# Two output tiles of a weight half, matmul by matmul in turn instead of one after the other

## The chip, the core and the metric

One core of a Trainium2 chip runs the whole kernel. The time is device microseconds of one execution. All times below come from the timed runs or from one profiled execution of the kernel before. The engines are named as in the profile: PE is TensorE's matmul, PEld its weight load, DVE is VectorE, ACT is ScalarE, POOL is GpSimd, SP is SyncE.

## The reference

One layer of a hybrid decoder on 336 tokens (16 meta tokens, 256 of a prompt, 8 sequences of 8 new ones), width 2048. Cut to what matters:

```python
def swiglu(x, wg, wu, wd):
    return (jax.nn.silu(x @ wg) * (x @ wu)) @ wd

def layer(h, st, p, lead):
    h = h + 0.5 * swiglu(rmsnorm(h, ...), w_gate, w_up, w_down)     # 2048 -> 5632 -> 2048
    z = rmsnorm(h, ...) @ w_in                                       # 2048 -> 8200
    y_s5, ... = s5_mixer(z[..., :o0], ...)                           # complex diagonal state space
    y_ml, ... = mlstm_mixer(...)                                     # matrix memory, 4 heads
    gates = sigmoid(z[..., o5:])
    merged = gates[..., :D] * (y_s5 @ w_branch_s5) + gates[..., D:] * (y_ml @ w_branch_mlstm)
    h = h + merged @ w_out
    h = h + 0.5 * swiglu(rmsnorm(h, ...), w_gate, w_up, w_down)
```

Everything is float32, and the outputs are the normed rows and the new states.

## The kernel before, in words

Activations lie by feature: a tile holds 128 features on the partitions and the tokens (336 in FFN 1 and the first part of the mixer, 320 after) along the free dimension. A float32 product is made of three matmuls of type float32r: high part of the weights times high part of x, high times low, low times high.

`Weights` (L47) brings the weights in the order of their use, in loads of 1 MB on SP's queue. Each load gives two halves of four k tiles by 256 columns. `_split` (L86) makes the two parts of a half: ACT copies `whi` (L95), DVE subtracts to get `wlo` (L96). `take` (L115) is called before a half's matmuls and splits two halves ahead (AHEAD = 2); four buffers each hold `whi` and `wlo`.

`product` (L380) adds one half to two PSUM tiles `ps[0]` and `ps[1]`, one for each 128 of its 256 columns. These are called column tile 0 and column tile 1 here. The matmuls are those of L388, L389 and L390, 24 to a half. After each column tile it calls `tick` (L407), which takes a step of the generators that run beside the products: `tick(0)` of those in `self.fast` alone, `tick(1)` of all in `self.bg`. The generator `s5_parameters` (in FFN 1, with `s5_weights`, L677, whose matmuls L751, L764 and L765 use small PSUM tiles) and `mlstm` (L1123) are in `fast`; `s5` (L1308), `v_turn` and others are not.

`pair` (L426) takes two PSUM tiles from the pool `psm` (four buffers, tag mm, in rotation; `mm_psum`, L142) and runs one to four halves into them. Small work uses another pool of four (`sm_psum`).

`ffn` (L432) goes over 11 blocks of 512 hidden features, each with two rounds `pr`. A round is a pair pg (gate, four halves) and a pair pu (up, four halves), and then `gated` (L438) for column tile 0 and for column tile 1:

```python
            nc.vector.tensor_tensor(gs, pg, self.rstd, op=ALU.mult)      # L443
            nc.scalar.activation(gs, gs, AF.Silu)                        # L444
            nc.vector.tensor_tensor(us, pu, self.rstd, op=ALU.mult)      # L445
            nc.vector.tensor_tensor(us, us, gs, op=ALU.mult)             # L446
            nc.scalar.copy(ah, us)                                       # L447
            nc.vector.tensor_tensor(al, us, ah.bitcast(F32), op=ALU.subtract)  # L448
```

The first round of each FFN uses the small pool for pg and pu; the other 21 use the mm pool. After the first round of a block comes `down` (L450) of the block before: eight pairs of one half each, after each of which `add` (L454) has DVE add both tiles to h (L457). At the end of FFN 1 the parts of the next norm are made as well (`ffn_done`, L330, L338). The mixer (L777) uses `pair` with two or four halves, and what reads its tiles is posted one to three halves later (`post`, L404).

The order of each engine's instructions is written out by the program (`manual_schedule`): an engine takes them as the Python code issues them.

Of the kernel before, what the change touches and what calls it, by code (L numbers as in the profile page):

```python
# [13 lines left out]
P = 128  # L14
# [32 lines left out]
class Weights:  # L47
    """The weights in the order in which TensorE takes them: loads of 1 MB, each cut into two halves
    of four k tiles by 256 columns, and each half split exactly into two float32r parts."""

# [51 lines left out]
    def first(self, part):  # L102
        """The first half, two k tiles at a time."""
        if part == 0:
            self.half[0] = tuple(self.k.wsp.tile([P, 4, 256], F32R, tag=t, name=t) for t in ("whi", "wlo"))
        s = slice(2 * part, 2 * part + 2)
        hi, lo = (t[:, s] for t in self.half[0])
        src = self.raw[0][:, s]
        self.k.nc.scalar.copy(hi, src)
        self.k.nc.vector.tensor_tensor(lo, src, hi.bitcast(F32), op=ALU.subtract)  # L110
        if part == 1:
            self.done[0] += 1
            self.split += 1
# [9 lines left out]
class Kernel:  # L123
# [43 lines left out]

# [1 line left out]
    def plan(self):  # L169
# [56 lines left out]

# [1 line left out]
    def constants(self):  # L228
# [89 lines left out]

# [1 line left out]
    def norm_begin(self, hi_slot, lo_slot, n, gain):  # L320
# [33 lines left out]

# [1 line left out]
    def load_x(self):  # L356
# [3 lines left out]
    def x_features(self, j):  # L360
        """Four tiles of x, turned and split; to be called again for what h takes from PSUM."""
        nc, xs = self.nc, self.xs
        tiles = []
        for m in range(4 * j, 4 * j + 4):
            ps = self.mm_psum()
            s = slice(P * m, P * m + P)
            nc.tensor.transpose(ps[:, 16:144], xs[0][:, s], self.ident)
            nc.tensor.transpose(ps[:, 144:272], xs[1][:, s], self.ident)
            nc.tensor.transpose(ps[:, 272:336], xs[2][0:64, s], self.ident[0:64, 0:64])
            nc.tensor.transpose(ps[:, 0:16], xs[2][64:80, s], self.ident[64:80, 64:80])  # L370
            self.norm_split(m, ps[:, 0:NT])
            tiles.append((m, ps))
            if m == 1:
                yield
        yield
        for m, ps in tiles:
            nc.vector.tensor_copy(self.h[:, m], ps[:, 0:NT])

# [1 line left out]
    def product(self, ps, half, xh, xl, k0, first, last, ks=range(4)):  # L380
        """Adds to the two PSUM tiles a half's four k tiles by its 256 columns."""
        nc = self.nc
        hi, lo = half
        for m in range(2):
            c = slice(P * m, P * m + P)
            for k in ks:
                a, b = xh(k0 + k), xl(k0 + k)
                nc.tensor.matmul(ps[m], hi[:, k, c], a, start=first and k == 0, stop=False)  # L388
                nc.tensor.matmul(ps[m], hi[:, k, c], b, start=False, stop=False)  # L389
                nc.tensor.matmul(ps[m], lo[:, k, c], a, start=False, stop=last and k == 3)  # L390
            if ks[-1] == 3:
                self.tick(m)

    def take(self):
        """The next half, and what was put off until now."""
        half = self.w.take()
        self.now += 1
        due = [x for x in self.posted if x[0] <= self.now]
        self.posted = [x for x in self.posted if x[0] > self.now]
        for _, fn in due:  # L400
            fn()
        return half
# [4 lines left out]
    def tick(self, m=1):  # L407
        """Takes what runs beside the large products a step further: at every half, and what is in
        fast at each of its two columns of tiles."""
        for g in list(self.bg):  # L410
            if m == 0 and g not in self.fast:
                continue
            try:
                next(g)
            except StopIteration:
                self.bg.remove(g)
# [122 lines left out]

# [1 line left out]
    def s5_parameters(self):  # L541
        nc, i = self.nc, self.ins
        v, s = nc.vector, nc.scalar
# [9 lines left out]
        at = [0]  # L553
# [21 lines left out]
        ps = self.sm_psum()  # L575
# [4 lines left out]
        ps = self.sm_psum()  # L580
# [10 lines left out]
        M, A, S = ALU.mult, ALU.add, ALU.subtract  # L591
# [32 lines left out]
        for j in range(1, 4):  # L624
            yield from cmul(pr[:, :, j], pi[:, :, j], pr[:, :, j - 1], pi[:, :, j - 1], pr[:, :, 0], pi[:, :, 0])
            yield
        # (Abar - 1) / A
        den, nr = take(32), take(32)
# [15 lines left out]
        for j in range(3):  # L644
            yield from cmul(er[:, :, 2 - j], ei[:, :, 2 - j], er[:, :, 3], ei[:, :, 3], pr[:, :, j], pi[:, :, j])
            yield
        # the phases of the slots, a step being four tokens
        p4r, p4i = take(32), take(32)
# [4 lines left out]
        for hv in range(2):  # L653
# [6 lines left out]
            while n < SL - 1:  # L660
                w = min(n, SL - 1 - n)
# [15 lines left out]
    def s5_weights(self, er, ei, pr, pi, decay4):  # L677
        """The matrices of four tokens' step, a group of four state tiles at a time."""
        nc, i = self.nc, self.ins
# [95 lines left out]

# [1 line left out]
    def mixer(self):  # L777
# [53 lines left out]
        self.drain(fin)  # L831
        # the gated linear unit
        yv = lambda t, s: (lambda k: t[:, k, s])
# [37 lines left out]

    # what was left in DRAM, a few tiles ahead
    def reload_begin(self, sources):
# [110 lines left out]
    def v_turn(self):  # L984
        """Turns v (head by head) so that tokens lie on the partitions."""
        nc = self.nc
        self.vt = [t[:, 0:768].rearrange("p (t c) -> p t c", t=3) for t in self.quarters(F32)]
        self.y_ml = []
        left = 8
        while left:  # L990
            if self.later and self.later[0][0] <= self.now:
                left -= 1
                _, m, v = self.later.pop(0)
                ps = self.sm_psum()
                for t, (at, n) in enumerate(((0, 128), (128, 128), (240, 96))):
                    nc.tensor.transpose(ps[0:n, P * t:P * t + P], v[:, at:at + n], self.ident)
                o = self.vt[m // 2][:, :, P * (m % 2):P * (m % 2) + P]
                nc.scalar.copy(o[:, 0:2], ps[:, 0:256].rearrange("p (t c) -> p t c", t=2))
                nc.vector.tensor_copy(o[0:96, 2], ps[0:96, 256:384])
            yield  # L1000
# [8 lines left out]

# [1 line left out]
    def gating_product(self, xh, xl):  # L1011
# [98 lines left out]
    def conv_out(self):  # L1110
        """The new rows of the convolution's buffer."""
        nc, s, a = self.nc, self.nc.scalar, self.aux
        self.cn_out = a[0:27, MLS:MLS + 1024]
        for b in range(2):
            ps = self.sm_psum()
            for m in range(4):
                nc.tensor.transpose(ps[0:27, P * m:P * m + P], self.cst[:, 4 * b + m], self.ident)
            s.copy(self.cn_out[0:27, 512 * b:512 * b + 512], ps[0:27])
        yield
        nc.gpsimd.dma_start(self.outs[7][0, 0], self.cn_out[0:3])  # L1120
        nc.gpsimd.dma_start(self.outs[13][0].rearrange("n r c -> (n r) c"), self.cn_out[3:27])

    def mlstm(self):  # L1123
# [37 lines left out]

        # columns of a score block, and of the live tokens they belong to
        blocks = ((0, 256, 0), (256, 400, 112), (400, 496, 224))
        load(3)
        for h in range(4):
# [29 lines left out]
            yield  # L1195
            # the new keys of four sequences, in two float32r parts, each twice
            for b in range(2):
# [6 lines left out]
                yield  # L1204
            # the denominator, on every partition
            den = self.sm_psum()
# [11 lines left out]
            for x in range(2):  # L1218
# [19 lines left out]
                yield  # L1238
                # the new memory
                up = self.sm_psum()  # L1240
# [22 lines left out]
            for x in range(2):  # L1263
                nc.gpsimd.dma_start(ob[:, x], self.o_dr[2 * h + x])
            # the new normaliser
            ps = self.sm_psum()
# [6 lines left out]
            tt(nt[:, 1:9, h], tn, ps[:, 2:10], A)  # L1273
            # the norm of a head, its gain and the output gate
            s.activation(sq, hh[:, 0], AF.Square)
# [23 lines left out]
    def contract(self, ps, dm, lhs, state):  # L1299
        """Sums over the tokens s of a score block, for the live tokens, and what the states give."""  # L1300
        pe = self.nc.tensor
# [4 lines left out]

# [1 line left out]
    def s5(self):  # L1308
# [23 lines left out]
        for g in range(NG):  # L1332
# [55 lines left out]
            yield  # L1388
        # the last states
        for a in range(2):  # L1390
# [15 lines left out]
    def s5_last(self):  # L1406
        """The skip, GELU, and the order of the tokens."""
        nc = self.nc
# [27 lines left out]

# [1 line left out]
    def before_end(self):  # L1438
# [93 lines left out]
```

## Time and profile before

| | |
|---|---|
| timed runs | 2798.72 and 2800.86 us, median 2799.79 |
| profiled execution, first to last instruction | 2797.4 us |
| TensorE matmul busy | 2776.8 us, 18640 instructions |
| VectorE busy | 1600.3 us, 2485 instructions |
| ScalarE busy | 1106.0 us, 1617 instructions |
| HBM | 163 GB/s over the span |

The profile tells its execution by its span alone; no separate time of that execution is given, so the timed runs stand beside it: they are 1.3 and 3.5 us above the span. Matmuls overlap in the records: a row of 0.31 us starts 0.15 us after the one before, so the time of one is read from the distance of the starts.

### The profile page before, as it was taken

What the parts mean: (1) busy time and instruction counts of PE and PEld (TensorE: products, weight loads), DVE (VectorE), ACT (ScalarE), POOL (GpSimd) and SP (SyncE); (2) the same over time, 40 slices, a digit from 0 to 9 for tenths busy, and PEclk for the clock granted to TensorE, in tenths of its full rate; (3) what the DMA queues carried; (4) which work ended last, traced back from release to release, by engine and by line L of the source; (5) the groups of instructions that cost most, each with busy time, mean ns of one, the idle gap of its engine ahead of it and who ended that gap; (6) DMA issues with size and microseconds to landing.
All of it is one profiled execution on the core that took longest, in us unless ns stands there. A gap on an engine that the chain in (4) does not pass through costs nothing.

```text
span 2797.4 us, 44767 instructions
## 1 busy us (share of the span) xinstructions
PE 2776.8 (99%) x18640; PEld 2759.9 (99%) x18640; DVE 1600.3 (57%) x2485; ACT 1106.0 (40%) x1617; POOL 194.5 (7%) x298
## 2 busy tenths in 40 slices
PE   9999999999999999999999999999999999999998
PEld 8999999999999999999999999999999999999998
DVE  6666565555544575767655556445445555445455
ACT  5433444444432353434344444443333333333334
POOL 4000001000000042000010100100000000000001
PEclk9999999999999999999999999999999999999999
DMA  6445544554444457566655666544444444454542
GB/s 183 148 137 179 156 160 159 186 166 158 157 165 141 140 178 197 188 197 203 205 166 170 204 200 206 172 148 151 151 152 150 151 151 147 142 164 137 165 146 88
DMA packets 375884, 459.03 MB, mean 164 GB/s; under 512 B 16338, under 2 KB 319422, under 8 KB 374641
## 3 DMA queue, kind: packets, MB, share of 16 engines
q1 hardware_dynamic: 360880, 417.33, 46.8%
q0 software_dynamic: 10336, 32.74, 3.4%
q10 hardware_dynamic: 4464, 6.09, 0.6%
q8 instruction: 147, 2.41, 0.4%
q14 instruction: 57, 0.46, 0.0%
HBM read 419.54 MB, written 36.57 MB: 163 GB/s over the span
## 4 chain that ended last, share of the span: by engine, by line
PE 97%; DVE 1%; ACT 1%; DMA 1%; issue 0%; SPq 0%; ACTq 0%; DVEq 0%
PE mm L388 30%; PE mm L390 30%; PE mm L389 30%; PE sm L388 1%; PE sm L390 1%; PE sm L389 1%; PE sm L1339 1%; PE sm L1232 0%; DVE slotB L330 0%; DVE wlo L96 0%; DMA aux<-u_dr 0%; PE sm L1384 0%; PE sm L765 0%; PE sm L1385 0%; PE sm L1225 0%
## 5 line engine op out<-in xcount | busy, mean ns | idle before, releaser
L96 DVE TENSOR_TENSOR wlo<-wraw,whi 128x1024 fp32r<-128x1024 f32 x727 | 881.9, 1225 | 653.5 <-ACT whi L95 652.8
L95 ACT CAST whi<-wraw 128x1024 fp32r<-128x1024 f32 x727 | 748.7, 1047 | 799.3 <-PE mm L389 774.3
L388 PE MATMUL mm<-slotA,whi 128*128 128x336 f32 (+1 forms) x2688 | 851.2, 317 | 0.3 <-DVE slotE L457 0.3
L390 PE MATMUL mm<-slotA,wlo 128*128 128x336 f32 (+1 forms) x2688 | 844.2, 314 | 0.0
L389 PE MATMUL mm<-slotB,whi 128*128 128x336 f32 (+1 forms) x2496 | 783.9, 314 | 0.0
L389 PE MATMUL mm<-quarter,whi 128*128 128x320 f32 (+1 forms) x1792 | 558.9, 312 | 0.0
L388 PEld LDWEIGHTS mm<-slotA,whi 128*128 128x128 f32 x2688 | 505.6, 188 | 2.8 <-issue 1.2
L390 PEld LDWEIGHTS mm<-slotA,wlo 128*128 128x128 f32 x2688 | 504.8, 188 | 0.2 <-DVE wlo L96 0.2
L388 PE MATMUL mm<-quarter,whi 128*128 128x320 f32 (+1 forms) x1536 | 481.2, 313 | 0.6 <-DVE slotE L457 0.6
L390 PE MATMUL mm<-quarter,wlo 128*128 128x320 f32 (+1 forms) x1536 | 480.4, 313 | 0.4 <-DVE wlo L96 0.4
L389 PEld LDWEIGHTS mm<-slotB,whi 128*128 128x128 f32 x2496 | 469.7, 188 | 1.2
L388 PE MATMUL mm<-slotB,whi 128*128 128x320 f32 x1472 | 455.1, 309 | 0.0
L390 PE MATMUL mm<-slotB,wlo 128*128 128x320 f32 x1472 | 454.8, 309 | 0.0
L389 PE MATMUL mm<-slotD,whi 128*128 128x320 f32 x1344 | 415.3, 309 | 0.0
L389 PEld LDWEIGHTS mm<-quarter,whi 128*128 128x128 f32 x1792 | 336.8, 188 | 0.0
L388 PEld LDWEIGHTS mm<-quarter,whi 128*128 128x128 f32 x1536 | 288.7, 188 | 1.1 <-issue 1.1
L390 PEld LDWEIGHTS mm<-quarter,wlo 128*128 128x128 f32 x1536 | 288.3, 188 | 0.8 <-DVE wlo L96 0.8
L388 PEld LDWEIGHTS mm<-slotB,whi 128*128 128x128 f32 x1472 | 276.3, 188 | 0.1
L390 PEld LDWEIGHTS mm<-slotB,wlo 128*128 128x128 f32 x1472 | 276.3, 188 | 0.0
L457 DVE SCALAR_TENSOR_TENSOR slotE<-mm,slotE 128x336 f32<-128x336 f32 (+1 forms) x352 | 171.4, 497 | 157.6 <-PE mm L390 148.7
L389 PEld LDWEIGHTS mm<-slotD,whi 128*128 128x128 f32 x1344 | 252.3, 188 | 0.1
L339 POOL TENSOR_TENSOR acc<-acc,sq 128x336 f32<-128x336 f32 (+1 forms) x58 | 61.1, 1054 | 1408.1 <-ACT sq L338 1406.1
(393 smaller groups left out, 1744.3 us busy)
## 6 DMA issues: line engine op xcount, KB each, us to landing
wraw<-in_ffn_w_down_dram SPq DMA_DIRECT2D x88, 1024.0 KB, 5.1
wraw<-in_ffn_w_gate_dram SPq DMA_DIRECT2D x87, 1024.0 KB, 5.1
wraw<-in_ffn_w_up_dram SPq DMA_DIRECT2D x87, 1024.0 KB, 5.1
wraw<-in_w_in_dram SPq DMA_DIRECT2D x64, 1024.0 KB, 5.7
wraw<-in_w_out_dram SPq DMA_DIRECT2D x16, 1024.0 KB, 5.5
w_dr<-slotD POOLq DMA_DIRECT2D x8, 1280.0 KB, 8.0
wraw<-in_w_branch_mlstm_dram SPq DMA_DIRECT2D x8, 1024.0 KB, 5.7
wraw<-in_w_branch_s_dram SPq DMA_DIRECT2D x8, 1024.0 KB, 5.5
```

The lines of the kernel that those rows point to most:

```text
L95: k.nc.scalar.copy(hi, src)
L96: k.nc.vector.tensor_tensor(lo, src, hi.bitcast(F32), op=ALU.subtract)
L339: nc.gpsimd.tensor_tensor(self.acc[:, 0:n], self.acc[:, 0:n], sq, op=ALU.add)
L388: nc.tensor.matmul(ps[m], hi[:, k, c], a, start=first and k == 0, stop=False)
L389: nc.tensor.matmul(ps[m], hi[:, k, c], b, start=False, stop=False)
L390: nc.tensor.matmul(ps[m], lo[:, k, c], a, start=False, stop=last and k == 3)
L457: nc.vector.scalar_tensor_tensor(hm, ps[m], 0.5, hm, op0=ALU.mult, op1=ALU.add)
L1339: pe.matmul(ps[:, NSL * t:NSL * t + NSL], w1[:, a, t], u4[g % 2][:, t], start=True, stop=True)
```

## The change

`product` is rewritten. For each k tile the three matmuls are issued for column tile 0 and column tile 1 in turn, and both calls of `tick` come after the last of the half's matmuls. The operands of each matmul and the order of the sums in each PSUM tile stay. The rest of the diff blanks comments and docstrings and moves no line.

```diff
     def product(self, ps, half, xh, xl, k0, first, last, ks=range(4)):
-        """Adds to the two PSUM tiles a half's four k tiles by its 256 columns."""
+
         nc = self.nc
         hi, lo = half
-        for m in range(2):
-            c = slice(P * m, P * m + P)
-            for k in ks:
-                a, b = xh(k0 + k), xl(k0 + k)
-                nc.tensor.matmul(ps[m], hi[:, k, c], a, start=first and k == 0, stop=False)
-                nc.tensor.matmul(ps[m], hi[:, k, c], b, start=False, stop=False)
-                nc.tensor.matmul(ps[m], lo[:, k, c], a, start=False, stop=last and k == 3)
-            if ks[-1] == 3:
+        cols = [slice(P * m, P * m + P) for m in range(2)]
+        for k in ks:
+            a, b = xh(k0 + k), xl(k0 + k)
+            for j, (w, x) in enumerate(((hi, a), (hi, b), (lo, a))):
+                for m, c in enumerate(cols):
+                    nc.tensor.matmul(ps[m], w[:, k, c], x, start=first and k == 0 and j == 0, stop=last and k == 3 and j == 2)
+        if ks[-1] == 3:
+            for m in range(2):
                 self.tick(m)
```

## Rows read from the trace of the kernel before

**Rows 1.** The page: busy time, TensorE's clock in 40 slices, the chain by engine.
```profile
PE 2776.8 (99%) x18640; PEld 2759.9 (99%) x18640; DVE 1600.3 (57%) x2485; ACT 1106.0 (40%) x1617; POOL 194.5 (7%) x298
...
PEclk9999999999999999999999999999999999999999
...
PE 97%; DVE 1%; ACT 1%; DMA 1%; issue 0%; SPq 0%; ACTq 0%; DVEq 0%
```

**Rows 2.** The page's groups (busy, mean ns, idle before): the split of the weights.
```profile
L96 DVE TENSOR_TENSOR wlo<-wraw,whi 128x1024 fp32r<-128x1024 f32 x727 | 881.9, 1225 | 653.5 <-ACT whi L95 652.8
```

**Rows 3.** Timeline of PE (start, duration in us) around the end of an up pair, FFN 2.
```profile
2071.27 0.31 PE L390 MATMUL mm<-slotB,wlo 128*128 128x320 f32 x1
2071.42 0.31 PE L388 MATMUL mm<-slotB,whi 128*128 128x320 f32 x1
...
2072.88 0.31 PE L389 MATMUL mm<-slotD,whi 128*128 128x320 f32 x1
2073.03 0.31 PE L390 MATMUL mm<-slotB,wlo 128*128 128x320 f32 x1
2073.18 0.31 PE L388 MATMUL mm<-slotB,whi 128*128 128x320 f32 x1
```

**Rows 4.** Timeline of DVE at the same place; in brackets the idle time before.
```profile
2071.62 0.49 DVE L445 TENSOR_TENSOR us<-mm,rstd 128x320 f32<-128x320 f32 x1 [2.72 <-PE mm L390]
...
2073.23 0.49 DVE L448 TENSOR_TENSOR quarter<-us,quarter 128x320 fp32r<-128x320 f32 x1 [0.53 <-ACT quarter L447]
2073.64 0.48 DVE L443 TENSOR_TENSOR gs<-mm,rstd 128x320 f32<-128x320 f32 x1
...
2076.63 3.50 DVE L96 TENSOR_TENSOR wlo<-wraw,whi 128x1024 fp32r<-128x1024 f32 x3 [0.46 <-ACT whi L95]
```

**Rows 5.** Lines L443 and L445 over the run: counts, and L445's waits.
```profile
L443 DVE TENSOR_TENSOR gs<-mm,rstd x84: 483/492/509, 77.7 to 2749.5; 128x336 f32<-128x336 f32 x42, 128x320 f32<-128x320 f32 x42
...
L445 DVE TENSOR_TENSOR us<-mm,rstd x84: 481/494/509, 81.2 to 2749.9; 128x336 f32<-128x336 f32 x42, 128x320 f32<-128x320 f32 x42
...
  PE mm L390: 99.6, 42
```

**Rows 6.** Timeline of PE in the first products.
```profile
12.20 0.48 PE L389 MATMUL sm<-slotB,whi 128*128 128x336 f32 x1
12.48 0.48 PE L390 MATMUL sm<-slotA,wlo 128*128 128x336 f32 x1
...
16.40 0.36 PE L389 MATMUL sm<-slotB,whi 128*128 128x336 f32 x1
```

**Rows 7.** Timelines of DVE and PE at the end of FFN 1, in `down`.
```profile
1018.45 0.50 DVE L457 SCALAR_TENSOR_TENSOR slotE<-mm,slotE 128x336 f32<-128x336 f32 x1
...
1019.09 0.39 PE L388 MATMUL mm<-quarter,whi 128*128 128x336 f32 x1 [0.28 <-DVE slotE L457]
1019.33 0.32 PE L389 MATMUL mm<-quarter,whi 128*128 128x336 f32 x1
1019.48 0.32 PE L390 MATMUL mm<-quarter,wlo 128*128 128x336 f32 x1
```

**Rows 8.** Timeline of DVE at the end of an up pair, FFN 1.
```profile
350.10 0.51 DVE L445 TENSOR_TENSOR us<-mm,rstd 128x336 f32<-128x336 f32 x1 [1.43 <-PE mm L390]
...
352.19 0.50 DVE L443 TENSOR_TENSOR gs<-mm,rstd 128x336 f32<-128x336 f32 x1
```

**Rows 9.** Timeline of PE there, and at the last such place.
```profile
349.75 0.32 PE L390 MATMUL mm<-slotA,wlo 128*128 128x336 f32 x1
...
351.76 0.30 PE L764 MATMUL sm<-slotD 128*128 128x32 f32 x2
...
353.46 0.40 PE L388 MATMUL mm<-slotA,whi 128*128 128x336 f32 x1
...
724.88 0.30 PE L764 MATMUL sm<-slotD 128*128 128x32 f32 x2
```

**Rows 10.** Timeline of DVE at another up pair of FFN 1.
```profile
201.70 0.51 DVE L446 TENSOR_TENSOR us<-us,gs 128x336 f32<-128x336 f32 x1 [0.46 <-DVE us L445]
```

**Rows 11.** Timelines of ACT and PE in mLSTM, first head.
```profile
1221.40 1.07 ACT L1226 COPY slotE<-sm 128x512 f32<-128x512 f32 x2 [0.40 <-PE sm L1225]
...
1227.69 1.51 PE L1232 MATMUL sm<-slotE 128*128 128x8 f32 x13
```

## The prediction

> **What bounds the kernel now.** I read the page's busy table and 40 slices first, then the chain. TensorE (PE) is busy 99% of the 2797.4 us span, its clock digit is 9 in every slice, and the chain that ended last is 97% PE [rows 1]. So PE has no slack, and whatever makes it wait lengthens the run by that much. Next comes the count of the work: every half of the weights is split once by L96, 727 times, and the very first half in two pieces by another line [rows 2]. That is 728 halves of 24 matmuls, 17472 matmuls.
>
> Third is the PE timeline at the end of an "up" pair of FFN 2 [rows 3]. Starts are 0.147 us apart (from 2071.27 to 2073.18 are 13 steps, 1.91 us). Column tile 0 ends with the matmul at 2071.27, tile 1 with the one at 2073.03, and the next pair starts at 2073.18. In FFN 1 (336 columns) a step is 0.1545 us.
>
> Fourth is the DVE timeline of the same place [rows 4]. After an up pair DVE runs `gated` for tile 0 and then for tile 1. Its L445 (the product with pu, tile 0) starts at 2071.62, 0.35 us after the start of tile 0's last matmul, having waited 2.72 us for it. Then come L446, L448 (behind a copy by ACT) and only then L443 of tile 1, which reads pg's second buffer from 2073.64 to 2074.12. The grouped view has 84 executions of L443 and of L445 on the mm pool, and 42 waits of L445 for PE [rows 5]: 42 pairs of `gated`, each with one wait, the one for tile 0.
>
> **The change part by part.**
>
> The alternation itself. Each of the 17472 matmuls is still issued, with its own weight load, on the same columns. What changes is that the PSUM bank switches at every matmul and the weights are never the same twice running. The trace has a bank switch at every tile boundary: 2071.27 to 2071.42 is 0.15 us, like 2072.88 to 2073.03 without one [rows 3]. So it costs 0. Bounds: at the half clock of the start a matmul of 336 columns takes 0.28 us [rows 6]; half of this, 0.140, would be the column time at full clock, so 0.0145 us per matmul could be gained at most (0.0145 x 17472 = 253 us). On the other side stands the 0.24 us after a restart [rows 7], 0.09 more per matmul. The boundary is the same event as the one that is added, so I take 0.
>
> The end of tile 0 moves. It was the 12th matmul of the last half and becomes the 23rd, 11 steps later. DVE takes its instructions in order, and L445 of tile 0 waits for that matmul, so all of `gated` shifts by 11 steps: 1.61 us in FFN 2, 1.70 in FFN 1. Behind the waiting L445 stand L446, L448, L443 of tile 1 and then the splits L96; ACT's copies of the next weights stand behind its own part of `gated`. The splits have room: the first one after it starts at 2076.63 [rows 4] and serves the third half from 2073.18, due 2 x 24 x 0.147 = 7.06 us after that, at 2080.2.
>
> The start of tile 1 moves. The pool has four mm buffers in rotation, pg has two and pu two, so the next pair writes pg's. That a pair waits for the readers of the pair two before is seen at the end of FFN 1, where the first matmul of a pair waits for L457 of the second pair before it [rows 7]. Before, pg's second buffer was first written by the 13th matmul of the next pair: with x the start of tile 0's last matmul, at x + 25 steps = x + 3.67 us, and L443 of tile 1 had ended at x + 2.85 (2074.12 - 2071.27): free by 0.8 us, so no wait shows. Now the second matmul writes it, due at x + 14 steps, and L443 ends at x + 11 steps + 2.85. From rows 7: PE starts 0.14 us after the end of the DVE instruction that it waits for (1018.95 to 1019.09), and its next matmul comes 0.24 us later where a step is 0.154, another 0.09. So the wait costs 2.85 + 0.14 + 0.09 - 3 steps:
> FFN 2: 3.08 - 0.44 = 2.64 us.
> FFN 1: x is 349.75, L443 of tile 1 ends at 352.69, so 2.94 + 0.23 - 0.46 = 2.71 us [rows 8, 9].
> Behind the waiting matmul stand all of PE's others; DVE and ACT, both far from full, only wait with it.
>
> Exceptions, all in FFN 1. At five of its 21 places the weights of S5 put 16 small matmuls between the two pairs, the first at 351.76 to 353.46, the last at 724.88 [rows 9]. They write other buffers and hide 1.70 us: 1.01 us is left of each. At one place L446 came 0.36 us late on DVE [rows 10]: 3.07 us.
> Sum: FFN 2 21 x 2.64 = 55.4; FFN 1 15 x 2.71 + 3.07 + 5 x 1.01 = 48.8; together 104.2 us.
>
> The other PSUM readers. `down` adds its two tiles after the pair instead of one in its middle; each buffer is needed a whole pair later (24 steps, 3.5 us) and two L457 take 0.91 us, so nothing shows, except at the end of FFN 1, where DVE is late already [rows 7]. There the second matmul must now await the second L457, 0.4 us on; but PE comes there 2.71 later and DVE only 1.70, so it may be less or more: 0, between -1.5 (the three waits of about half a microsecond gone) and +3. The mixer's pairs have two to four halves until their buffers return: 0. At the very end both L457 follow the last matmul, where one preceded it: +0.4.
>
> The background steps. tick(0) now comes after tile 1, so two steps of what is in `fast` follow one another. `product` issues only matmuls, hence no other engine's order changes, nor SP's or POOL's queue; only these steps' small matmuls move, at most 12 steps (1.8 us) later. Operations two steps apart keep one whole half between them, as before: ACT's copies for the mLSTM state ended by 1222.47 and are first used at 1227.69 [rows 11]. Three steps may shrink to one half. In mlstm a head has 8 such groups of matmuls, 32 in all; if each lost 1.8 us it would be 57 us; below nothing it cannot go, since PE waits at none of them now. The row shows 5 us of room, so 0.
>
> Total: 104.2 + 0.4 = 104.6 us on the profiled span, 2902.0 us. The timed runs stand 1.3 to 3.5 us above that span, the median 2.4, so the time is 2904 us.
>
> **A rule that speaks against the change.** In the trace the clock stays at its upper level, 2.4 GHz, throughout [rows 1], but PE never idles 1 us there; so what waits of over 2 us do, no row shows. The Trainium skill (TensorE: Matmul & The Clock Gate, "A second HAM failure mode: psum-queue depth-cycling") reports a kernel that cycled through PSUM banks in each iteration, whose matmul groups were separated by small idle times, and whose clock went back and forth between its levels. It gives no price; the case by it is the second rival.
>
> **The rivals.**
> 1. The buffer is free in time (the wait isn't where I put it, or something moves L443 forward): about 2800 us. For it: PE waits at none of these places now. Against: DVE is in order and L443 of tile 1 stands behind L445 of tile 0 in all 42.
> 2. Each wait lets the clock fall to 1.2 GHz. At the start the products ran at that level from 12.20 to 16.40 us, 15 steps of 0.28 us [rows 6], 15 x 0.1255 = 1.9 us more than at the upper one. 42 x 1.9 = 80 us on top: 2984 us, and more if it stays down longer. Against: 2.4 us of idleness stands in 28 us of dense work or more.
> 3. The other side: writing one bank twice running is what makes a matmul 0.147 instead of about 0.133 us, and taking turns frees it. At the full 0.0145 us it is 253 us less: 2651 us. It breaks even at 104.6 / 17472 = 0.0060 us a matmul, and is faster by 2% from 0.0092. Against: the boundary step of 0.15 us.
> 4. The doubled background steps stall PE in mlstm too: 2904 + 57 = 2961 us at worst.
>
> **How the numbers follow.** Forecast 0.79; rival 1 0.05; rival 2 0.07; rival 3 0.03; rival 4 0.06. The likeliest case alone reaches from 2890 (the waits a sixth smaller) to 2925 (a fifth larger). The range takes in most of rival 4 as well: 2885 to 2945. A measurement tells 2% (56 us) from no change: faster 0.03 (rival 3), same 0.05 (rival 1), slower 0.92.
>
> **What would show it.** Right: PE's second matmul of the next pair, line L388 or its successor, waits for DVE L443 42 times, idle about 2.4 us each (0.25 of the cost lies in the modelled end and the restart), 5 of them under 1 us, some 93 us in all; PE's busy share falls to about 96%; L445's 42 waits for PE grow from 99.6 by 42 x 1.65 to about 169 us; steps stay 0.147 and 0.1545 us; the clock stays full. Wrong: another step within a half (rival 3), a clock digit under 9 (rival 2), waits of PE in the mLSTM stretch (rival 4), no waits for L443 (rival 1).

## The result, and the profile after

The changed kernel takes 2825.9 us (2825.42 and 2826.38) against 2799.79: 1.0096 of the time before, 95% interval 1.008 to 1.0112. It is slower, as forecast, but by 26 us and not by 104: outside the stated range, and within the 2% that the prediction called "same" and gave 0.05.

The page of the changed kernel, against [rows 1]:

```profile
span 2824.6 us, 44746 instructions
...
PE 2791.8 (99%) x18640; PEld 2762.2 (98%) x18640; DVE 1588.9 (56%) x2485; ACT 1104.4 (39%) x1617; POOL 194.6 (7%) x298
...
PEclk9999999999999999999999999999999999999999
...
PE 96%; DVE 1%; DMA 1%; SPq 0%; ACT 0%; issue 0%; ACTq 0%; DVEq 0%
```

The span grew by 27.2 us, PE is still full at the upper clock, and DVE has 1% of the chain, as before. What PE waits for (waits of engine PE: us in total, times, longest):

```profile
PE mm L389 <- DVE us L445: 10.8, 37, 0.3
...
PE sm L1225 <- ACT slotE L1226: 0.7, 1, 0.7
PE mm L389 <- DVE wlo L96: 0.6, 2, 0.3
PE mm L389 <- DVE gs L443: 0.4, 2, 0.2
```

There are 37 waits for L445, which is 42 less the five places with small matmuls between the pairs. But L445 is of tile 0, where L443 of tile 1 was forecast, and the idle time is 0.29 us each, not 2.4. (The two waits for L443 come 11 matmuls further on, in the last block of each FFN.) The same place of FFN 2 as [rows 3, 4], first PE and then DVE:

```profile
2089.74 0.46 PE L389 MATMUL mm<-slotB,wlo 128*128 128x320 f32 x2
2090.03 0.31 PE L389 MATMUL mm<-slotB,whi 128*128 128x320 f32 x1
2090.63 0.41 PE L389 MATMUL mm<-slotB,whi 128*128 128x320 f32 x1 [0.29 <-DVE us L445]
2090.88 0.31 PE L389 MATMUL mm<-slotD,whi 128*128 128x320 f32 x1
```
```profile
2090.08 0.49 DVE L445 TENSOR_TENSOR us<-mm,rstd 128x320 f32<-128x320 f32 x1 [4.48 <-PE mm L389]
...
2092.10 0.48 DVE L443 TENSOR_TENSOR gs<-mm,rstd 128x320 f32<-128x320 f32 x1
```

The matmuls of 2089.74 are the 23rd and 24th of pu's last half (x2, 0.147 apart). The next pair's first matmul starts on time at 2090.03. Its second is due at 2090.18 and starts at 2090.63, 0.06 us after the end of L445 (2090.08 + 0.49). L443 of tile 1 runs until 2092.58, long after that. The wait is 0.45 us, and 2090.88 is 0.25 after 2090.63 where a step is 0.147, another 0.10: 0.55 us.

Where the 27.2 us come from I worked out from the starts of the first matmul of every half in both traces (the 728 differences, one trace minus the other). The difference grows in jumps:

| where | jumps | us |
|---|---|---|
| after up pairs, FFN 1 (15 places) and FFN 2 (20) | 0.55 to 0.57 each | 19.5 |
| the last block of each FFN | 1.22 and 1.21 | 2.4 |
| the five places with L764 between the pairs | none | 0 |
| one step of mLSTM, in the half that starts at 1345 us of the trace before | 0.88 | 0.9 |
| `down` after the second up pair, 121 to 125 us | 0.46 and 0.27 | 0.7 |
| spread over the halves with 336 columns, 3.0 of it in FFN 1 | about 0.01 each | 3.3 |
| other | | 0.4 |

### The profile page after: what moved, and what is told of

It reads as the page before. It is cut to its first block, busy times and chain, and to the rows that moved or that the text cites. A ratio compares the mean times of both kernels' runs of the same rounds, so it can differ in the third digit from the quotient of the medians.

```text
span 2824.6 us, 44746 instructions
## 1 busy us (share of the span) xinstructions
PE 2791.8 (99%) x18640; PEld 2762.2 (98%) x18640; DVE 1588.9 (56%) x2485; ACT 1104.4 (39%) x1617; POOL 194.6 (7%) x298
## 4 chain that ended last, share of the span: by engine, by line
PE 96%; DVE 1%; DMA 1%; SPq 0%; ACT 0%; issue 0%; ACTq 0%; DVEq 0%
PE mm L389 89%; PE sm L389 2%; DVE us L445 1%; PE sm L1339 0%; PE sm L1232 0%; PE sm L1225 0%; PE sm L1383 0%; PE sm L765 0%; PE sm L1385 0%; PE sm L1384 0%; PE sm L751 0%; PE sm L1242 0%; DMA aux<-y_dr 0%; DMA aux<-g_dr 0%; PE sm L764 0%; DMA aux<-in_x_sample_dram 0%
## 5 line engine op out<-in xcount | busy, mean ns | idle before, releaser
L389 PE MATMUL mm<-slotB,whi 128*128 128x320 f32 (+1 forms) x3968 | 908.8, 313 | 2.9 <-DVE us L445 2.9
L389 PEld LDWEIGHTS mm<-slotB,whi 128*128 128x128 f32 x3968 | 668.8, 188 | 5.7 <-DVE us L445 5.5
L389 PE MATMUL mm<-quarter,whi 128*128 128x320 f32 (+1 forms) x3328 | 653.8, 314 | 6.7 <-DVE us L445 5.8
L389 PE MATMUL mm<-slotA,whi 128*128 128x336 f32 (+1 forms) x2752 | 647.2, 318 | 2.1 <-DVE us L445 2.0
L389 PE MATMUL mm<-slotA,wlo 128*128 128x336 f32 (+1 forms) x2688 | 625.8, 314 | 0.0
L389 PEld LDWEIGHTS mm<-quarter,whi 128*128 128x128 f32 x3328 | 533.2, 188 | 14.8 <-DVE us L445 11.4
L389 PEld LDWEIGHTS mm<-slotA,wlo 128*128 128x128 f32 x2688 | 456.3, 188 | 0.0
L389 PE MATMUL mm<-quarter,wlo 128*128 128x320 f32 (+1 forms) x1536 | 355.6, 313 | 0.6 <-DVE wlo L96 0.6
L389 PE MATMUL mm<-slotB,wlo 128*128 128x320 f32 x1472 | 335.3, 309 | 0.0
L389 PE MATMUL mm<-slotD,whi 128*128 128x320 f32 x1344 | 306.2, 309 | 0.0
L457 DVE SCALAR_TENSOR_TENSOR slotE<-mm,slotE 128x336 f32<-128x336 f32 (+1 forms) x352 | 159.1, 494 | 151.6 <-PE mm L389 150.6
L445 DVE TENSOR_TENSOR us<-mm,rstd 128x336 f32<-128x336 f32 (+1 forms) x84 | 41.6, 495 | 175.4 <-PE mm L389 175.4
L444 ACT ACTIVATE gs<-gs 128x336 f32<-128x336 f32 (+1 forms) x88 | 42.1, 478 | 123.5 <-DVE gs L443 123.5
L448 DVE TENSOR_TENSOR quarter<-us,quarter 128x336 fp32r<-128x336 f32 (+1 forms) x88 | 44.0, 500 | 46.9 <-ACT quarter L447 46.9
```

The costliest lines, as they stand in the source:

```text
L389: nc.tensor.matmul(ps[m], w[:, k, c], x, start=first and k == 0 and j == 0, stop=last and k == 3 and j == 2)
L457: nc.vector.scalar_tensor_tensor(hm, ps[m], 0.5, hm, op0=ALU.mult, op1=ALU.add)
```

## The experiments

**Which buffer the next pair gets.** Theory after the result: the PSUM pool doesn't rotate; it gives its buffers out in the order in which their last readers stand in the program. `gated` reads pg's tile 0, pu's tile 0, pg's tile 1, pu's tile 1. So the next pair gets pg's first buffer and pu's first buffer, and its second matmul waits for L445 of tile 0. The compiled program lists the bank of each PSUM tile; of the changed kernel, in program order, from the second block of FFN 1 on:

```
pg         banks 0, 1
pu         banks 3, 2
down q=0   banks 0, 3
down q=1   banks 1, 2
down q=2   banks 0, 3
```

The compiled kernel before has the same list. That shows where the buffers are, not what they cost. Two runs change one side of it each.

The changed kernel with both pg tiles read first:

```diff
...                                        # gate(): the first two lines of gated() by themselves
-                for m in range(2):
-                    gated(f + m, pg[m], pu[m])
+                gs = [gate(pg[m]) for m in range(2)]       # L443 and L444
+                for m in range(2):
+                    gated(f + m, gs[m], pu[m])             # L445 to L448
```

> The changed kernel, but DVE reads both pg tiles (L443 of tile 0 and of tile 1) before it reads either pu tile. Theory: the PSUM pool gives its buffers out in the order in which their last readers stand in the program, so the pair after an up pair now gets pg's two buffers, both free long before, and the waits of 0.56 us for L445 are gone at all 35 plain places; the two last blocks may wait some 1.3 us each for pu's second buffer; 2803 to 2808 us. Rival A: PE waits for L445 for another reason than the buffer (a semaphore that stands for all of DVE's work so far): about 2826 us or more, with the same 37 waits. Rival B: the buffers rotate, as the prediction had it, and something else hid L443: 2826 us or less, with no wait for L443 but waits for L445 unchanged.

It took 2804.98 us, 1.0025 of before (1.0014 to 1.0035). What PE still waits for there (L448 in that kernel is L445, the product with pu):

```profile
PE mm L389 <- DVE us L448: 1.1, 2, 0.5
```

Of the 37 waits two are left, the two last blocks (jumps of 0.80 and 0.82 us, less than I expected). In the list of banks of this kernel pg has 0 and 3, pu 1 and 2, and `down` q=0 has 0 and 3, pg's two. So 21 us of the 26 hung on the order in which two tiles are read. Rivals A and B fall: DVE does the same work, and L445 of tile 0 still comes late, while PE's waits for it are gone. At the place shown above it waits 4.08 us for PE, with L443 of tile 1 now done ahead of it; in the changed kernel it was 4.48, before 2.72. In DVE's timeline of e1:

```profile
2077.10 0.49 DVE L448 TENSOR_TENSOR us<-mm,rstd 128x320 f32<-128x320 f32 x1 [4.08 <-PE mm L389]
```

The changed kernel with the rotation that the prediction assumed, four pools of one buffer each:

```diff
-        self.psm = pool("psm", 4, space=bass.MemoryType.PSUM)
+        self.psm = [pool(f"psm{j}", 1, space=bass.MemoryType.PSUM) for j in range(4)]
+        self.turn = 0
...
-        return self.psm.tile([P, 512], F32, tag="mm", name="mm")
+        self.turn += 1
+        return self.psm[(self.turn - 1) % 4].tile([P, 512], F32, tag="mm", name="mm")
```

The norm's one tile takes the next buffer without moving the turn on.

> The changed kernel, with four PSUM pools of one buffer each that are handed out in fixed rotation, so the pair after an up pair gets pg's two buffers while gated keeps its order (L443 of tile 1 after L445, L446 and L448 of tile 0). Theory: the prediction's sum was right for a rotation, and only the buffer was wrong: the second matmul of the next pair waits for L443 of tile 1, 2.64 us in FFN 2 and 2.71 in FFN 1, 104 us in all, with the 5 us that the changed kernel shows beside its waits about 2905 us (2895 to 2915), 42 waits for L443. Rival A (the wait is for DVE in general, whatever buffer): 2826 us. Rival B: waits of over 2 us let the clock fall: 2980 us or more, with a granted clock under 0.99.

It took 2933.98 us, 1.0483 (1.0466 to 1.0501), and PE now waits for L443 (L448 in that kernel) at all 42 places:

```profile
PE mm L394 <- DVE gs L448: 89.5, 42, 2.7
```

The jumps against the trace before are 2.57 us at twelve places of FFN 2 and 2.64 at five of FFN 1 (forecast 2.64 and 2.71); four of the five places with small matmuls show 0.85 to 0.87 (forecast 1.01). So the prediction's sum was nearly right for a rotation. At the 21 other places the jump is 1.5 us larger: 3.93 to 4.43 instead of 2.6 at 20 of them, and 2.41 at the fifth place with small matmuls. One of them, PE's timeline and the stretches around it with the granted clock:

```profile
2004.92 0.31 PE L394 MATMUL mm<-quarter,whi 128*128 128x320 f32 x1
2007.53 1.17 PE L394 MATMUL mm<-quarter,whi 128*128 128x320 f32 x3 [2.30 <-DVE gs L448]
2008.50 0.73 PE L394 MATMUL mm<-quarter,wlo 128*128 128x320 f32 x2
```
```profile
2000.00:2004.90 4.90, 4.90 (x35) 1.00 0.64 216
2007.50:2010.90 3.40, 3.37 (x12) 0.50 0.00 0
2011.50:2015.00 3.50, 3.50 (x26) 1.00 0.00 0
```

PE idled 2.30 us, and the 3.40 us behind it ran at 1.2 GHz: 12 matmuls, where the 3.50 us after them hold 26 (both counts take in those that reach into the stretch). The trace has 21 such falls before the last product, one for each larger jump, 21 x 1.53 = 32 us. That is why this run is 19 us above the expected range: rival 2 of the prediction, in half of the places. The mean granted clock of the run was 0.986 (0.998 in the kernel before).

The same rotation with the matmuls in the old order:

> The kernel before, with the four mm buffers in fixed rotation (as in e2_rotation, but the matmuls in the old order). Theory: pg's second buffer is due 13 matmuls into the next pair, 0.8 us after L443 of tile 1 has ended, so the rotation costs nothing in the old order: within 0.2% of the kernel before, no waits for L443. If rotation itself cost something, e2's 2934 us would not be the price of the alternation: 2820 us or more.

2799.79 us, 1.0003 (0.9994 to 1.0012), no wait for L443. Rotation costs nothing by itself in the old order: in this trace pg's second buffer is written 0.8 us after L443 of tile 1 has ended, as the prediction worked out.

**Which end of a pair matters.** Two runs restore the old order in one half of each pair:

```diff
+        for both in ((0,), (1,)) if first else ((0, 1),):     # the other run: if last
             for k in ks:
...
-                for m, c in enumerate(cols):
-                    nc.tensor.matmul(ps[m], w[:, k, c], x, ...)
+                    for m in both:
+                        nc.tensor.matmul(ps[m], w[:, k, cols[m]], x, ...)
```

> The changed kernel, but in the first half of every pair the two tiles are made one after the other, as before; the last half of a pair of several halves still takes turns (a pair of one half is in the old order). Theory: the wait needs both the late end of tile 0 and the early start of tile 1; here the second buffer is due 11 steps (1.6 us) later, and L445 of tile 0 ends 1.2 us before that: no waits, 2801 to 2806 us. Rival C: the late end of tile 0 alone costs (DVE and the splits fall behind): 2820 us or more.

> The changed kernel, but in the last half of every pair the two tiles are made one after the other, as before; the first half of a pair of several halves still takes turns. Theory: tile 0 ends 11 steps (1.6 us) earlier than in the changed kernel, so L445 of tile 0 has ended when the next pair's second matmul is due: no waits, 2801 to 2806 us. Rival D: the early start of tile 1 alone costs: 2820 us or more, with waits for DVE at the second matmul.

2807.28 us, 1.0034 (1.0023 to 1.0046), and 2802.02 us, 1.0011 (1.0001 to 1.002). In both the waits for L445 are gone, so the wait needs the late end of tile 0 and the early start of tile 1 together, and either alone is nearly free. The first is 1.3 us above what I expected. Its profile has waits of PE that I had not counted: for the sums of `down` (L458 there is L457), for L443 (L444 there) in the two last blocks, and for a load of the mLSTM state. Three of the five waits for the sums of `down` are those of the kernel before [rows 7], and the wait for the load is in e7 below too; what makes the others appear was not followed further:

```profile
PE mm L390 <- DVE slotE L458: 2.1, 5, 0.9
...
PE mm L390 <- DVE gs L444: 1.5, 2, 0.8
PE sm L1226 <- DMA aux<-in_state_mlstm_C_dram: 1.4, 1, 1.4
```

**The order of the reads in the old order.**

> The kernel before, with both pg tiles read before either pu tile (as in e1_gates_first, but the matmuls in the old order). Theory: PE waited at none of these places, so nothing changes: within 0.15% of the kernel before. Rival E: e1's gain is that the other order of gated is faster as such, and not the buffer: some 20 us less than before.

2798.98 us, 1.0000 (0.9991 to 1.001). Reading both pg tiles first brings nothing where PE didn't wait; rival E falls.

**What is left, 5 to 7 us.** The ticks alone, with the matmuls in the old order:

```diff
-            if ks[-1] == 3:
-                self.tick(m)
+        if ks[-1] == 3:
+            for m in range(2):
+                self.tick(m)
```

> The kernel before with its matmuls in the old order, and only the other part of the change: both calls of tick after the second tile. Theory: the part of the change that is no wait for L445 (5 of its 27 us) is in part this: 2799 to 2803 us, with the largest single step in the mLSTM stretch, 0.9 us at about 1345 us. Rival: the ticks cost nothing and all 5 us come with the alternation: 2798.4, no step there.

2802.23 us, 1.0012 (1.0004 to 1.0021). The step of 0.89 us, in the half that starts at 1345 us of the trace before, is there. In the kernel before the eight transposes of L1225 stand in one row, 2 us behind the matmul of L1256; now they follow it at once, and the second four wait for ACT's copy of the first four (PE's timeline; L1226 and L1227 in that kernel are L1225 and L1226):

```profile
1348.37 0.60 PE L1226 MATMUL sm<-ident,slotE 128*128 128x128 f32 x4
1349.65 0.55 PE L1226 MATMUL sm<-ident,slotE 128*128 128x128 f32 x3 [0.68 <-ACT slotE L1227]
```

A second step, 1.28 us in the half that starts at 1438 us, is a wait for a load of the mLSTM state; the changed kernel doesn't have it, so I don't count it to the change. In the profiled spans the ticks are 1.3 us (2798.7 against 2797.4), in the medians 3.7 against the before of that series (2798.53); 0.9 us of it is shown to be theirs. (The profiled execution, 2800.53 us, is one of the faster ones of this kernel's 2799.07 to 2805.48.)

The alternation without the doubled steps and without the wait, e1's kernel with tick(0) after 12 of the 24 matmuls:

```diff
+            if ks[-1] == 3 and k == ks[len(ks) // 2 - 1]:
+                self.tick(0)
         if ks[-1] == 3:
-            for m in range(2):
-                self.tick(m)
+            self.tick(1)
```

> e1_gates_first with tick(0) in the middle of a half, after 12 of the 24 matmuls, and tick(1) at its end: the alternation without the doubled steps and without the wait for L445. Theory: alternation as such is free, and what is left of e1's 6 us over the kernel before is the two last blocks (0.8 us each) and small shifts: 2800 to 2804 us, without the step of 0.9 us at about 1345 us. Rival: alternation has a price of its own in every matmul: 2805 us as in e1_gates_first, or more.

2804.65 us, 1.0021 (1.0012 to 1.003): the step of 0.9 us is gone, but the time is nearly that of e1. In the profiled spans e1 has 4.9 us more than the kernel before and this run 4.4. So most of what is left comes with the alternation and not with the ticks. The two last blocks are 1.6 us of it. Another part is in every matmul of 336 columns. The mean distance between the starts of successive matmuls of `product` (those under 0.2 us), from the records:

| | 100 to 1000 us, 336 columns | 1900 to 2700 us, 320 columns |
|---|---|---|
| before | 154.43 ns | 146.67 ns |
| e7, old order, ticks moved | 154.43 ns | 146.67 ns |
| e9, in turn, ticks apart | 154.95 ns | 146.67 ns |
| the changed kernel | 154.95 ns | 146.65 ns |
| e4, in turn in the last three halves of gate and up pairs alone | 154.75 ns | 146.67 ns |
| e5, in turn in the first three halves of these pairs alone | 154.74 ns | 146.67 ns |

Half a nanosecond on the 5,600 matmuls that the first column counts is 2.9 us, and in e4 and e5, where half of FFN 1's matmuls are in turn, the excess is 0.3. It is a mean: at 336 columns the distance depends on the matmul's place among the 24 of a half, from 152.5 to 158.3 ns before and from 149.6 to 163.5 in the changed kernel, while at 320 it is 146.5 to 146.7 at every place in both. So it isn't one price for each change of the bank, since in the changed kernel the bank changes at every place. Why the pattern is there at 336 columns and not at 320 stays open; no run tried another width.

No run points to a version that beats the kernel before: those without the wait end at 1.0011 to 1.0034 of it, and those in the old order at 1.0000 to 1.0012.

## Why the prediction was wrong

**The step that failed** is in "The start of tile 1 moves": "The pool has four mm buffers in rotation, pg has two and pu two, so the next pair writes pg's." ("In rotation" in the section on the kernel before is the same mistake.) The next pair writes pg's first and pu's first, in the kernel before too. What it awaits is therefore the first DVE instruction after tile 0's end (L445) and not the fourth (L443 of tile 1): 0.55 us a place instead of 2.64, 22 us instead of 104. [rows 7], which I took as evidence for the rotation, can't tell the two apart: `add` reads its two tiles one after the other, so the order of release is there the order of a rotation. The order of reads in `gated`, quoted above the prediction, was what mattered.

**What held.** The alternation is free at 320 columns, as taken from the tile boundary [rows 3], and costs 0.5 ns at 336, 3.3 us in all where 0 was taken, inside the bounds of +90 and -14.5 ns. The end of tile 0 moved by 11 steps: L445's 42 waits for PE grew from 99.6 [rows 5] to 175.4 us (169 was forecast). The five places with small matmuls hide the wait, here wholly, since 0.56 is less than their 1.70 us. The restart costs 0.10 us, 0.09 was forecast from [rows 7]. With the rotation restored, the cost came out 0.07 us below the forecast at the 17 plain places where the clock didn't fall, and 0.14 to 0.16 below at four of those with small matmuls. The 0.07 is in the start after a wait: PE starts 0.05 to 0.06 us after the end of the DVE instruction, where 0.14 had been taken from [rows 7]. The other PSUM readers were put at 0, with bounds of -1.5 to +3 for the end of FFN 1 alone: 0.7 us came at 121 to 125 us, in a `down` where nothing was to show, and the up pairs of both last blocks gave 1.2 us instead of 2.6. The background steps were put at 0 with a bound of 57: one step of 0.9 us, for a copy in the transposes, which [rows 11] doesn't show.

**Sums and readings.** The sums come out as they stand, but for "a sixth smaller", which gives 2887 and not 2890. That the clock stays at its upper level "throughout" is too wide: the first products run at 0.28 us a matmul [rows 6], and the granted clock is 1.2 GHz in the last 9 us, where PE has no matmul. And PE does idle over 1 us, 4.3 and 1.6 us for loads in the first 8 us; from the first product on its longest wait is 0.74 us. None of this enters the sum.

**The rivals.** Rival 1 (the buffer is free in time) had half of the truth: another buffer, due at the same moment, is free 2 us sooner, but still 0.45 us too late. It needed a third value, the wait for L445, between "no wait" and "2.64 us"; I priced only the ends. Rival 2 didn't happen in the changed kernel, where PE idles 0.29 us, and did at 21 of the 42 places in e2. Rival 3 didn't: no mean step became shorter by more than 0.02 ns. Rival 4 is the 0.9 us.

## What to carry to other kernels

Which buffer a tile pool gives next follows from the order in which the program releases them, so when a change moves the first write of a tile, follow the buffers in the program and don't assume a rotation. Where two accumulators are made in turn, both end late and both are wanted early: the reads behind them should free first what is ready first, here both gate tiles ahead of the up tiles, which took 21 of the 26 us away. A row that fits two hypotheses bears on neither; look for the place where they differ.

## What the runs showed that I had not expected

The clock: in e2 PE idled 2.3 to 2.7 us at 37 places. The granted clock fell to 1.2 GHz around 20 of them and stayed at 2.4 GHz at the other 17, though up pairs of the same length came before each. The 21st fall came at one of the five places with small matmuls, behind 1.7 us of these and a wait of 0.59 us; the other four, with waits of 0.58 us, show none. PE's timeline and the stretch with the granted clock:

```profile
573.42 0.42 PE L394 MATMUL mm<-slotA,whi 128*128 128x336 f32 x1 [0.59 <-DVE gs L448]
```
```profile
573.95:577.35 3.40, 3.40 (x14) 0.50 0.00 0
```

A fall cost 1.5 us on top of the wait, and what decides between a fall and none no run shows. The changed kernel's 37 waits of 0.29 us never brought the clock down. The page of the Trainium skill that the prediction weighs (TensorE: Matmul & The Clock Gate, "A second HAM failure mode: psum-queue depth-cycling") tells of a kernel whose clock goes back and forth because small idle times stand often enough between its groups of matmuls. This agrees with e2, by the 21 falls at 42 waits; the changed kernel, with the same groups and waits of 0.29 us, shows no fall before its last product.

Taking turns between two banks at every matmul neither gained nor cost anything at 320 columns (146.67 ns in both orders) and cost 0.5 ns at 336.
